# Moving the small tiles of a hybrid decoder kernel so that matmul operands and weights start at multiples of 512 bytes in SBUF

## The chip, the cores and the metric

The kernel runs on one NeuronCore of a Trainium2 chip. The metric is the device time of one execution in microseconds. The kernel before took 1934.75 us, the median of three runs (1932.48 to 1936.17).

## The reference

Two decoder layers over 256 tokens of width 2048, all in float32:

```
layer 0:  h = h + pool_mixer(rmsnorm(h))       # 4 channel groups, trailing means over 2/4/8/16 tokens, 512x512 product
          h = h + swiglu(rmsnorm(h))           # w_gate, w_up: 2048 x 5632; w_down: 5632 x 2048
layer 1:  h = h + diff_attention(rmsnorm(h))   # 8 heads, two softmaxes per head (128 wide), v 256 wide, ALiBi bias
          h = h + swiglu(rmsnorm(h))
out = rmsnorm(h)
diff_attention: a = softmax(q1 k1) - lam * softmax(q2 k2);  o = rmsnorm(a v) * subln_g * (1 - lambda_init);  o w_o
lam = exp(lq1 . lk1) - exp(lq2 . lk2) + lambda_init
```

## The kernel before

**The products.** Every large product is made of float32r matmuls of 128x128 stationary and up to 512 moving columns. An operand is held as a high and a low float32r part, and a product is three matmuls: high x high, high x low, low x high. Weights come from HBM as tiles `raw` of 128 x 4 x 512 floats, 1 MB each, by SP's queue (`load`, L102). ScalarE casts a tile to `whi`, VectorE subtracts to `wlo` (`halves`, L107). Three buffers of each of the three exist, so that loads and casts run some tiles ahead of TensorE.

**group (L130)** does a run of weight tiles into PSUM banks. A plain step multiplies the two 128-column blocks of one weight tile's four quarters with the operand tile: 24 matmuls of 512 moving columns at L164, the activation tile stationary, the weight moving. A step in `SEVEN` (three of the eight w_gu steps) uses seven products in place of eight: VectorE makes sums of the weight quarters (`tsum`, L116 to L119), ScalarE and VectorE split them to `thi` and `tlo` (L122, L123), and 21 matmuls follow, 12 of them with thi or tlo.

**The stages.** The start loads x, computes the pooling mixer and its square sums. Each FFN goes in three chunks of 4, 4 and 3 groups of 512 columns: w_gu (stationary: xq, tiles named xp in the trace), then transposes of h (L361) and the split into the tiles named h (`h0_0` to `h3_1`), then w_down with the h tiles stationary. Attention computes q and k of head after head in `product` (L418 with 512 moving columns, L420 with 256; here the weight is stationary and xp moves), scores and softmax, then w_v (xp stationary), the value products, and w_o with the tiles oT stationary.

**Where tiles lie.** A pool's tiles are laid one after the other in SBUF in the order in which they are first asked for, each place rounded up to 32 bytes; the pools `const`, `resid`, `wraw`, `whl` and `tmp` follow one another, and the pools of a stage (`start`, `ffn0`, `attn`, `ffn1`) begin where they end. So a small tile moves all that comes after it. `const` holds gain_sb (384 bytes a partition), subln_sb (8), lam_sb (16), dist_sb (1024), ident and ones (512 each). Of the tile `warm`, which ScalarE alone writes, there are two buffers in `tmp`.

**The order of the work.** The framework's scheduler orders each engine's instructions ahead of the run, from dependences and priorities in the order of the code. SP issues its loads in the order so found; a load waits until its buffer is free.

Of the kernel before, what the change touches and what calls it, by code (L numbers as in the profile page):

```python
# [9 lines left out]
F32 = mybir.dt.float32  # L10
# [6 lines left out]
P = 128  # L17
S = 256
# [26 lines left out]
def trunk_kernel(ctx, tc, x_t, x_n, gains, scale_in, final_in, subln, lam_in, band, dist,  # L45
# [10 lines left out]
    nc = tc.nc  # L56

    const = ctx.enter_context(tc.tile_pool(name="const", bufs=1))
# [3 lines left out]
    tmp = ctx.enter_context(tc.tile_pool(name="tmp", bufs=2))  # L62
# [14 lines left out]


    gain_sb = const.tile([P, 6, NK], F32, name="gain_sb")
    subln_sb = const.tile([P, 2], F32, name="subln_sb")  # L80
    lam_sb = const.tile([P, 4], F32, name="lam_sb")
    dist_sb = const.tile([P, 2 * P], F32, name="dist_sb")
    ident = const.tile([P, P], F32, name="ident")
    ones = const.tile([P, P], F32, name="ones")
# [113 lines left out]
    def rsqrt(ss, n, cols):  # L198


        v, s, t, r = (tmp.tile([P, 8], F32, name=f"rs_{x}") for x in "vstr")
        v, s, t, r = v[:, :cols], s[:, :cols], t[:, :cols], r[:, :cols]
        nc.vector.tensor_scalar(v, ss, 1.0 / n, EPS, ALU.mult, ALU.add)
        nc.scalar.activation(s, v, AF.Sqrt)
        nc.vector.reciprocal(s, s)
        nc.vector.tensor_tensor(t, s, s, ALU.mult)
        nc.vector.scalar_tensor_tensor(t, t, -0.5, v, ALU.mult, ALU.mult)
        nc.vector.scalar_tensor_tensor(r, t, 1.5, s, ALU.add, ALU.mult)
        return r

    def square_sum(ss, t, j):

        sq = tmp.tile([P, 512], F32, name="sq", bufs=1)
        nc.scalar.activation(sq, x_tok[:, t, j * 512:(j + 1) * 512], AF.Square, accum_out=ss[:, t, j:j + 1])  # L214

    def row_scale(ss):
        tot = tmp.tile([P, 2], F32, name="ss_tot")
        nc.vector.tensor_reduce(tot, ss, AX.X, ALU.add)
        r = tmp.tile([P, 2], F32, name="r_tok", bufs=3)
        nc.vector.tensor_copy(r, rsqrt(tot, D, 2))  # L220
        return r
# [35 lines left out]
    with tc.tile_pool(name="start", bufs=1, reuse_waits="tile") as st:  # L257
# [2 lines left out]
        xf = st.tile([P, NK, S], F32, name="xf")  # L260
        nc.scalar.dma_start(out=gain_sb, in_=gains)

        warm = tmp.tile([P, 8], F32, name="warm")
        nc.scalar.activation(warm[:, 0:1], ones[:, 0:1], AF.Sqrt)
        wp = aux()
        for _ in range(WARM):
# [55 lines left out]
        r = row_scale(ss_in)  # L322
        nc.sync.dma_start(out=band_sb, in_=band)
        nc.sync.dma_start(out=scale_sb, in_=scale_in)
        nc.sync.dma_start(out=subln_sb, in_=subln)
        nc.sync.dma_start(out=lam_sb, in_=lam_in)
        nc.sync.dma_start(out=dist_sb, in_=dist)
        group_product(2)
        group_mean(0)
# [5 lines left out]
    def ffn(layer, xq, ss, seven, next_op, next_gain):  # L335
# [3 lines left out]
        with tc.tile_pool(name=f"ffn{layer}", bufs=1, reuse_waits="tile") as hp:  # L339
            g0 = 0  # L340
            for c, n in enumerate(CHUNKS):
# [6 lines left out]
                for g in range(g0, g0 + n):  # L348
                    ps = group([(xq[p], p in seven, w_gu[layer][g, p]) for p in range(NP)], hp)
                    cs = combined(ps, hp)  # L350
                    h = hp.tile([P, 2, 512], F32, name="h")
# [14 lines left out]
                for o in range(2):  # L366
                    if last and o == 1:

                        pre = tmp.tile([P, 8], F32, name="warm")
                        nc.scalar.activation(pre[:, 0:1], x_tok[:, 0, 0:1], AF.Square)  # L370
                        nc.scalar.activation(pre[:, 0:1], pre[:, 0:1], AF.Sqrt)
                    ps = group([(hp_tiles[i], False, w_down[layer][o, 2 * g0 + i]) for i in range(2 * n)])
                    cs = combined(ps, hp)
                    for b in range(2):
                        j = 2 * o + b
                        for t in range(2):
                            cols = slice(j * 512, (j + 1) * 512)
                            nc.vector.tensor_tensor(x_tok[:, t, cols], cs[t][b], x_tok[:, t, cols], ALU.add)
                            if last:
                                square_sum(ss_next, t, j)  # L380
                        if last and next_op is not None:
                            transposed(next_op, j, next_gain)
                g0 += n
            if next_op is None:

                r = row_scale(ss_next)
                for j in range(4):
                    cols = slice(j * 512, (j + 1) * 512)
                    y = hp.tile([P, 2, 512], F32, name="y", tag=f"h{j // 2}_{j % 2}")
                    for t in range(2):  # L390
# [4 lines left out]
                        out=out[:, cols].rearrange("(t p) n -> p t n", p=P), in_=y)  # L395
        return ss_next

    xp = operand()
    ss = ffn(0, xq, ss, SEVEN, xp, 3)


    ss_next = tmp.tile([P, 2, 4], F32, name="ss")
    with tc.tile_pool(name="attn", bufs=1, reuse_waits="tile") as ap_, ExitStack() as heads:
        at = heads.enter_context(tc.tile_pool(name="attn_tmp", bufs=2, reuse_waits="tile"))
        v_sb = ap_.tile([P, 2, D], F32, name="v_sb")
        r_col = row_scale(ss)
        qs_col = ap_.tile([P, 2], F32, name="qs_col")
        nc.vector.tensor_scalar(qs_col, r_col, QK_SCALE, None, ALU.mult)
        r = None
        neg_lam = None  # L410
# [31 lines left out]
        probs = None  # L442
        for h in range(H):

            qk = ap_.tile([P, 4, S], F32, name=f"qk{h}", tag="qk", bufs=8)
            for i in range(4):
                ps = product(w_qk[h * 4 + i], acts)
                if i == 1 and probs is not None:
# [87 lines left out]
        for g in range(2):  # L536
            cs = combined(group([(oT[p], False, w_o[g, p]) for p in range(NP)]))
            for b in range(2):
# [5 lines left out]
                transposed(xq, j, 4, SEVEN)  # L544

    ffn(1, xq, ss_next, SEVEN, None, None)


# [89 lines left out]
```

## Time and profile before

| | |
|---|---|
| median of three runs | 1934.75 us (1932.48 to 1936.17) |
| the profiled execution | 1936.85 us, of which the span of instructions is 1935.1 |
| mean granted TensorE clock | 0.992 of full |
| TensorE matmul busy | 1892.9 us, 8508 recorded matmuls |
| VectorE busy | 1345.3 us |
| ScalarE busy | 921.5 us |
| read from HBM | 355.39 MB, 185 GB/s |

A matmul's recorded length contains its way through the array, so the lengths of matmuls that follow each other overlap. How fast the stream runs is read from the distance between starts, in the timeline or in a window's count.

### The profile page before, as it was taken

The page shows a single profiled execution, that of the slowest core. Times are in us where ns is not written, and L with a number is a line of the kernel's source. Part 1 is how long each engine was busy: PE and PEld are TensorE (multiplying, and loading weights), DVE is VectorE, ACT ScalarE, POOL GpSimd, SP SyncE. Part 2 cuts the span into 40 slices and gives each one's busy share as a digit, 9 for nine tenths or more (in the row PEclk, how much of TensorE's full clock was granted, in tenths as well). Part 3 has the DMA queues.
Part 4 walks back from the last instruction along what each step waited for, and adds up shares of the span by engine and source line. Part 5 has one row for each costly group of instructions (what it writes and reads, how often), then busy time and mean ns, then how long its engine had stood idle before and what let it go on. Part 6 is the DMA issues. An engine that isn't in the chain of part 4 may idle for free.

```text
span 1935.1 us, 20835 instructions
## 1 busy us (share of the span) xinstructions
PE 1892.9 (98%) x8508; PEld 1528.9 (79%) x8508; DVE 1345.3 (70%) x1311; ACT 921.5 (48%) x892; POOL 0.7 (0%) x6
## 2 busy tenths in 40 slices
PE   8899999999999999999999999999999999999997
PEld 5678878888888887888887777788888888888885
DVE  5889746888557974666654356888557887468854
ACT  5555534455334545544445544555334554335542
POOL 0000000000000000000000000000000000000000
PEclk9999999999999999999999999999999999999999
DMA  7455555555555454555553354555555556565552
GB/s 281 152 196 196 196 180 193 193 196 198 193 185 207 174 210 163 177 174 177 177 186 127 135 174 155 194 195 196 197 193 196 196 176 216 178 213 196 197 194 87
DMA packets 51151, 358.83 MB, mean 185 GB/s; under 512 B 6000, under 2 KB 6256, under 8 KB 8432
## 3 DMA queue, kind: packets, MB, share of 16 engines
q1 hardware_dynamic: 50080, 355.36, 52.7%
q10 hardware_dynamic: 976, 2.15, 0.3%
q8 instruction: 66, 1.08, 0.2%
q14 instruction: 29, 0.24, 0.0%
HBM read 355.39 MB, written 2.10 MB: 185 GB/s over the span
## 4 chain that ended last, share of the span: by engine, by line
PE 93%; DVE 3%; ACT 2%; DMA 1%; issue 1%; SPq 0%; DVEq 0%; ACTq 0%
PE b L164 80%; PE b L418 6%; PE b L420 3%; PE b L361 1%; DVE wlo L111 1%; DMA x_tok<-x_n 1%; ACT whi L110 1%; PE b L299 1%; PE b L485 1%; ACT sq L214 0%; PE b L531 0%; PE b L309 0%; DVE xp L226 0%; DMA raw<-w_gu 0%; DVE y L391 0%
## 5 line engine op out<-in xcount | busy, mean ns | idle before, releaser
L111 DVE TENSOR_TENSOR wlo<-raw,whi 128x2048 fp32r<-128x2048 f32 (+1 forms) x331 | 721.4, 2183 | 367.5 <-ACT whi L110 367.3
L110 ACT CAST whi<-raw 128x2048 fp32r<-128x2048 f32 (+1 forms) x331 | 603.7, 1827 | 625.0 <-PE b L164 528.2
L164 PE MATMUL b<-whi,xp 128*128 128x512 f32 x2412 | 770.4, 393 | 6.4 <-DVE xp L226 3.9
L164 PEld LDWEIGHTS b<-whi,xp 128*128 128x128 f32 x2412 | 453.1, 188 | 106.6 <-issue 4.8
L164 PE MATMUL b<-wlo,xp 128*128 128x512 f32 x1206 | 472.1, 391 | 1.7 <-DVE wlo L111 1.6
L164 PE MATMUL b<-whi,h 128*128 128x512 f32 x1408 | 446.9, 397 | 0.0
L164 PEld LDWEIGHTS b<-whi,h 128*128 128x128 f32 x1408 | 264.0, 188 | 65.1 <-DVE h L364 2.0
L164 PE MATMUL b<-wlo,h 128*128 128x512 f32 x704 | 278.5, 396 | 0.0
L164 PEld LDWEIGHTS b<-wlo,xp 128*128 128x128 f32 x1206 | 227.1, 188 | 51.5 <-DVE wlo L111 3.0
L164 PE MATMUL b<-thi,xp 128*128 128x512 f32 x528 | 186.9, 401 | 2.1 <-ACT thi L122 2.1
L123 DVE TENSOR_TENSOR tlo<-tsum,thi 128x2048 fp32r<-128x2048 f32 x66 | 151.1, 2290 | 52.4 <-ACT thi L122 51.7
L418 PE MATMUL b<-xp,whi 128*128 128x512 f32 x512 | 183.0, 401 | 0.0
L122 ACT CAST thi<-tsum 128x2048 fp32r<-128x2048 f32 x66 | 126.2, 1912 | 99.8 <-DVE tsum L119 77.0
L164 PEld LDWEIGHTS b<-wlo,h 128*128 128x128 f32 x704 | 132.3, 188 | 31.5 <-DVE wlo L111 0.4
L420 PE MATMUL b<-xp,wlo 128*128 128x256 f32 x512 | 137.9, 280 | 0.0
L164 PEld LDWEIGHTS b<-thi,xp 128*128 128x128 f32 x528 | 96.7, 188 | 29.7 <-ACT thi L122 10.4
L418 PEld LDWEIGHTS b<-xp,whi 128*128 128x128 f32 x512 | 95.0, 188 | 19.7
L164 PE MATMUL b<-tlo,xp 128*128 128x512 f32 x264 | 105.6, 400 | 0.0
L420 PEld LDWEIGHTS b<-xp,wlo 128*128 128x128 f32 x512 | 96.6, 189 | 2.6
L164 PE MATMUL b<-whi,oT 128*128 128x512 f32 x256 | 82.7, 402 | 0.4 <-DVE xp L226 0.4
L116 DVE TENSOR_TENSOR tsum<-raw 128x1024 f32<-128x1024 f32 x66 | 80.6, 1221 | 0.6
L164 PEld LDWEIGHTS b<-tlo,xp 128*128 128x128 f32 x264 | 49.5, 188 | 14.0 <-DVE tlo L123 2.6
(122 smaller groups left out, 1022.7 us busy)
## 6 DMA issues: line engine op xcount, KB each, us to landing
raw<-w_gu SPq DMA_DIRECT2D x176, 1024.0 KB, 4.9
raw<-w_down SPq DMA_DIRECT2D x88, 1024.0 KB, 4.9
raw<-w_qk SPq DMA_DIRECT2D x32, 1024.0 KB, 4.8
raw<-w_v SPq DMA_DIRECT2D x16, 1024.0 KB, 4.9
raw<-w_o SPq DMA_DIRECT2D x16, 1024.0 KB, 4.8
raw<-pool_w SPq DMA_DIRECT2D x3, 1024.0 KB, 11.1
x_tok<-x_n SPq DMA_DIRECT2D x1, 2048.0 KB, 14.8
xf<-x_t SPq DMA_DIRECT2D x3, 512.0 KB, 11.3
```

Of the source, the lines that this page charges most:

```text
L110: nc.scalar.copy(hi[:, lo_block:], raw[:, lo_block:])
L111: nc.vector.tensor_tensor(lo[:, lo_block:], raw[:, lo_block:], f32(hi[:, lo_block:]), ALU.subtract)
L116: nc.vector.tensor_tensor(t[:, T1:T3 + 1], raw[:, B11:B22 + 1], raw[:, B12:B12 + 1].broadcast_to([P, 2, 512]), ALU.add)
L122: nc.scalar.copy(hi, t)
L123: nc.vector.tensor_tensor(lo, t, f32(hi), ALU.subtract)
L164: nc.tensor.matmul(ps[b], x, y[:, block], start=first, stop=(left[b] == 0))
L299: nc.tensor.matmul(zp[g][t], u, w[:, k % 4], start=(k % 4 == 0 and i == 0), stop=(k % 4 == 3 and i == 2))
L361: nc.tensor.transpose(tp[:, k, t * P:(t + 1) * P], h[:, t, (2 * i + k) * P:(2 * i + k + 1) * P], ident)
L418: big = lambda: nc.tensor.matmul(ps.rearrange("p a s -> p (a s)"), hi[:, k], a.rearrange("p a s -> p (a s)"), start=(k == 0), stop=(k == N ...
L420: small = lambda: nc.tensor.matmul(ps[:, 0, :], lo[:, k], a[:, 0, :], start=False, stop=False)
L485: nc.tensor.matmul(sc[:, :nk], qk[:, c, qb * P:(qb + 1) * P], qk[:, 2 + c, :nk], start=True, stop=True)
```

## The change

The two small tiles subln_sb and lam_sb leave the pool `const` and are made in the pool of the attention stage, behind the first of the eight qk buffers and qs_col; their two loads are issued there in place of at the start. The first qk tile is asked for before qs_col, so that the eight qk places (used again for oT) start the part of the pool behind v_sb. The tile `warm` has one buffer.

```diff
--- before.py
+++ after.py
@@ -77,8 +77,6 @@
 
 
     gain_sb = const.tile([P, 6, NK], F32, name="gain_sb")
-    subln_sb = const.tile([P, 2], F32, name="subln_sb")
-    lam_sb = const.tile([P, 4], F32, name="lam_sb")
     dist_sb = const.tile([P, 2 * P], F32, name="dist_sb")
     ident = const.tile([P, P], F32, name="ident")
     ones = const.tile([P, P], F32, name="ones")
@@ -260,7 +258,7 @@
         xf = st.tile([P, NK, S], F32, name="xf")
         nc.scalar.dma_start(out=gain_sb, in_=gains)
 
-        warm = tmp.tile([P, 8], F32, name="warm")
+        warm = tmp.tile([P, 8], F32, name="warm", bufs=1)
         nc.scalar.activation(warm[:, 0:1], ones[:, 0:1], AF.Sqrt)
         wp = aux()
         for _ in range(WARM):
@@ -322,8 +320,6 @@
         r = row_scale(ss_in)
         nc.sync.dma_start(out=band_sb, in_=band)
         nc.sync.dma_start(out=scale_sb, in_=scale_in)
-        nc.sync.dma_start(out=subln_sb, in_=subln)
-        nc.sync.dma_start(out=lam_sb, in_=lam_in)
         nc.sync.dma_start(out=dist_sb, in_=dist)
         group_product(2)
         group_mean(0)
@@ -366,7 +362,7 @@
                 for o in range(2):
                     if last and o == 1:
 
-                        pre = tmp.tile([P, 8], F32, name="warm")
+                        pre = tmp.tile([P, 8], F32, name="warm", bufs=1)
                         nc.scalar.activation(pre[:, 0:1], x_tok[:, 0, 0:1], AF.Square)
                         nc.scalar.activation(pre[:, 0:1], pre[:, 0:1], AF.Sqrt)
                     ps = group([(hp_tiles[i], False, w_down[layer][o, 2 * g0 + i]) for i in range(2 * n)])
@@ -404,7 +400,12 @@
         at = heads.enter_context(tc.tile_pool(name="attn_tmp", bufs=2, reuse_waits="tile"))
         v_sb = ap_.tile([P, 2, D], F32, name="v_sb")
         r_col = row_scale(ss)
+        qk = ap_.tile([P, 4, S], F32, name="qk0", tag="qk", bufs=8)
         qs_col = ap_.tile([P, 2], F32, name="qs_col")
+        subln_sb = ap_.tile([P, 2], F32, name="subln_sb")
+        nc.sync.dma_start(out=subln_sb, in_=subln)
+        lam_sb = ap_.tile([P, 4], F32, name="lam_sb")
+        nc.sync.dma_start(out=lam_sb, in_=lam_in)
         nc.vector.tensor_scalar(qs_col, r_col, QK_SCALE, None, ALU.mult)
         r = None
         neg_lam = None
@@ -442,7 +443,8 @@
         probs = None
         for h in range(H):
 
-            qk = ap_.tile([P, 4, S], F32, name=f"qk{h}", tag="qk", bufs=8)
+            if h:
+                qk = ap_.tile([P, 4, S], F32, name=f"qk{h}", tag="qk", bufs=8)
             for i in range(4):
                 ps = product(w_qk[h * 4 + i], acts)
                 if i == 1 and probs is not None:
```

The first byte of the tiles in a partition, modulo 512, as the built programs have it:

| tiles | before | after |
|---|---|---|
| raw, whi, wlo; all xp and xq; x_tok; ident, ones | 64 | 0 |
| tsum, thi, tlo; h and the h tiles of w_down; band_sb, z, w0, x0; v_sb; e | 96 | 0 |
| qk and oT | 128 | 0 |
| aT | 256 | 224 |
| q_c, k_s, bias, s_sb | 256 | 224 |

Every row or block that a matmul reads lies at a multiple of 512 bytes behind the start of its tile in the products of L164 and L418, so the table holds for the operands as well.

The scheduler's order changes at two places. SP's queue at the start, before (a row is line, operation, tile written and read, shape, count):

```order
L317 DMA x_tok<-x_n 128x4096
L323 DMA band_sb<-band 128x1536
L324 DMA scale_sb<-scale_in 128x2048
L325 DMA subln_sb<-subln 128x2
L326 DMA lam_sb<-lam_in 128x4
L327 DMA dist_sb<-dist 128x256
L104 DMA raw<-pool_w 128x2048
```

SP's queue there after the change, with the line numbers of the changed kernel:

```order
L315 DMA x_tok<-x_n 128x4096
L321 DMA band_sb<-band 128x1536
L322 DMA scale_sb<-scale_in 128x2048
L323 DMA dist_sb<-dist 128x256
L102 DMA raw<-pool_w 128x2048
```

The two small loads are gone from between scale_sb and dist_sb, and the third load of pool_w is two places further up.

SP's queue around the attention stage after the change; before, the 32 loads of w_qk stand there without a break:

```order
L102 DMA raw<-w_gu 128x2048 x24
L102 DMA raw<-w_down 128x2048 x12
L102 DMA raw<-w_qk 128x2048 x5
L406 DMA subln_sb<-subln 128x2
L408 DMA lam_sb<-lam_in 128x4
L102 DMA raw<-w_qk 128x2048 x27
```

The small loads now go out behind the fifth load of w_qk.

VectorE at the end of the first FFN, before (lp and gs are what lam_sb and subln_sb are read for):

```order
L378 TENSOR_TENSOR x_tok<-b_5070,x_tok 128x512
L459 TENSOR_TENSOR lp<-lam_sb 128x2
L467 TENSOR_SCALAR gs<-subln_sb 128x2
L477 TENSOR_SCALAR bias<-dist_sb 128x256 x2
L111 TENSOR_TENSOR wlo<-raw,whi 128x2048
L226 SCALAR_TENSOR_TENSOR xp<-b_5233,gain_sb,xp 128x256
```

VectorE there after the change:

```order
L224 SCALAR_TENSOR_TENSOR xp<-b_5253,gain_sb,xp 128x256
L216 TENSOR_REDUCE ss_tot<-ss 128x2
L461 TENSOR_TENSOR lp<-lam_sb 128x2
L469 TENSOR_SCALAR gs<-subln_sb 128x2
L201 TENSOR_SCALAR rs_v<-ss_tot 128x2
```

lp and gs stand ten operations later, behind the two of bias, the wlo of a weight tile, six splits of xp and ss_tot. At the start, one split of xp (out of four) on ScalarE and VectorE stands one place earlier, ahead of a square sum and of an addition to x_tok. Elsewhere each engine's order is what it was.

## Rows read from the trace of the kernel before

**Rows 1.** The page of the profile, part 1: busy time of each engine, its share of the span, and its instructions.
```profile
PE 1892.9 (98%) x8508; PEld 1528.9 (79%) x8508; DVE 1345.3 (70%) x1311; ACT 921.5 (48%) x892; POOL 0.7 (0%) x6
```

**Rows 2.** The page, part 4: the chain of work that ended last, its shares by engine.
```profile
PE 93%; DVE 3%; ACT 2%; DMA 1%; issue 1%; SPq 0%; DVEq 0%; ACTq 0%
```

**Rows 3.** The groups of instructions of the whole span with shapes kept apart: line, engine, operation, tiles, shapes and count, then busy time in us, the mean of one in ns, and the engine's idle time before them in us. Lines of other groups stand where the dots are.
```profile
L164 PE MATMUL b<-whi,xp 128*128 128x512 f32 x2412 | 770.4, 393 | 6.4 <-DVE xp L226 3.9 <-ACT whi L110 1.7 <-ACT xp L250 0.7
L164 PE MATMUL b<-wlo,xp 128*128 128x512 f32 x1206 | 472.1, 391 | 1.7 <-DVE wlo L111 1.6
...
L164 PE MATMUL b<-whi,h 128*128 128x512 f32 x1408 | 446.9, 397 | 0.0
L164 PE MATMUL b<-wlo,h 128*128 128x512 f32 x704 | 278.5, 396 | 0.0
...
L164 PE MATMUL b<-thi,xp 128*128 128x512 f32 x528 | 186.9, 401 | 2.1 <-ACT thi L122 2.1
...
L164 PE MATMUL b<-tlo,xp 128*128 128x512 f32 x264 | 105.6, 400 | 0.0
...
L164 PE MATMUL b<-whi,oT 128*128 128x512 f32 x256 | 82.7, 402 | 0.4 <-DVE xp L226 0.4
L164 PE MATMUL b<-wlo,oT 128*128 128x512 f32 x128 | 51.1, 399 | 0.0
```

**Rows 4.** Three windows (us from the span's start), with the instructions of line L164 alone: length, busy time and count of TensorE's matmuls and of its weight loads, granted clock, DMA share, GB/s.
```profile
1000.00:1028.00 28.00, 28.00 (x125) 23.09 (x123) 1.00 0.60 221
250.00:320.00 70.00, 70.00 (x302) 56.36 (x301) 1.00 0.56 195
1112.00:1138.00 26.00, 26.00 (x113) 20.97 (x112) 1.00 0.59 201
```

**Rows 5.** A window over four whole groups of w_gu in the first FFN, all engines: length, then busy time (and count) of matmuls, weight loads, VectorE, ScalarE and POOL, granted clock, DMA share, GB/s.
```profile
328.37:499.26 170.89, 170.89 (x757) 139.04 (x756) 143.29 (x117) 88.93 (x64) 0.00 (x0) 1.00 0.56 197
```

**Rows 6.** The timeline of TensorE at transposes inside a w_gu group: start and length in us, instruction and count (equal ones that follow each other are one row).
```profile
415.98 0.82 PE L361 MATMUL b<-ident,h 128*128 128x128 f32 x6
416.55 0.48 PE L164 MATMUL b<-tlo,xp 128*128 128x512 f32 x1
416.87 0.39 PE L164 MATMUL b<-thi,xp 128*128 128x512 f32 x1
```

**Rows 7.** The timeline of TensorE in w_v, columns as in Rows 6. Between the dots the rows of one and of two take turns without a break.
```profile
1000.02 0.61 PE L164 MATMUL b<-whi,xp 128*128 128x512 f32 x2
1000.47 0.39 PE L164 MATMUL b<-wlo,xp 128*128 128x512 f32 x1
...
1003.42 0.61 PE L164 MATMUL b<-whi,xp 128*128 128x512 f32 x2
```

**Rows 8.** The same in w_o.
```profile
1120.13 0.63 PE L164 MATMUL b<-whi,oT 128*128 128x512 f32 x2
1120.60 0.40 PE L164 MATMUL b<-wlo,oT 128*128 128x512 f32 x1
...
1123.63 0.63 PE L164 MATMUL b<-whi,oT 128*128 128x512 f32 x2
```

**Rows 9.** The same in w_gu, where whi gives way to thi.
```profile
152.65 0.39 PE L164 MATMUL b<-whi,xp 128*128 128x512 f32 x1
152.87 0.40 PE L164 MATMUL b<-thi,xp 128*128 128x512 f32 x1
153.11 0.39 PE L164 MATMUL b<-tlo,xp 128*128 128x512 f32 x1
153.34 0.40 PE L164 MATMUL b<-thi,xp 128*128 128x512 f32 x1
```

**Rows 10.** The same at the pooling product of the start, in plain float32; one product is two recorded passes.
```profile
54.87 1.02 PE L309 MATMUL b<-z,band_sb 128*128 128x512 f32 x2
55.73 1.02 PE L311 MATMUL b<-z,band_sb 128*128 128x512 f32 x2
```

**Rows 11.** The same in the QK products; L418 has 512 moving columns, L420 has 256. The two lines take turns between the dots.
```profile
799.80 0.40 PE L418 MATMUL b<-xp,whi 128*128 128x512 f32 x1
800.04 0.28 PE L420 MATMUL b<-xp,wlo 128*128 128x256 f32 x1
...
801.92 0.40 PE L418 MATMUL b<-xp,whi 128*128 128x512 f32 x1
```

**Rows 12.** What TensorE waited for between 75 and 1935 us: total in us, times, longest.
```profile
PE b L164 <- ACT thi L122: 2.1, 2, 1.1
PE b L164 <- ACT whi L110: 1.7, 2, 1.1
```

**Rows 13.** The timeline of SP's queue (the DMA issues) at the start.
```profile
8.82 0.33 SPq L325 DMA_DIRECT2D subln_sb<-subln  x1
...
13.83 0.33 SPq L104 DMA_DIRECT2D raw<-pool_w  x1
```

**Rows 14.** The timeline of VectorE at the start of the attention layer.
```profile
789.63 0.15 DVE L459 TENSOR_TENSOR lp<-lam_sb 128x2 f32<-128x2 f32 x1
```

**Rows 15.** The timeline of SP's queue there: the fifth load of w_qk.
```profile
787.74 0.33 SPq L104 DMA_DIRECT2D raw<-w_qk  x1
```

**Rows 16.** The page, part 6: DMA issues of one kind, KB each, median us from issue to landing.
```profile
raw<-w_qk SPq DMA_DIRECT2D x32, 1024.0 KB, 4.8
```

## Prediction

> **What bounds the kernel now.** I read the busy times first. The reader is to see that TensorE is busy for 98% of the span while VectorE has 70% and ScalarE 48% [rows 1], and that 93% of the chain that ended last is TensorE [rows 2]. So a change pays here only if it shortens TensorE's own stream, and by as much as the stream shrinks, unless another engine then comes last. Its waits on the casts after the start come to 2.1 and 1.7 us [rows 12], so there is little waiting to win.
>
> The second view is the list of matmul groups with shapes kept apart [rows 3]. All eight groups of L164 are the same instruction (128x128 stationary, 512 columns moving), yet the mean of one is 391 to 393 ns with xp and whi/wlo, 396 and 397 with h, 399 to 402 with oT, and 400 and 401 with thi/tlo. The recorded time of one contains its latency, so the distance between starts has to be read elsewhere.
>
> The third view is the timeline in steady stretches. In w_v, with xp stationary, a triple (whi twice, wlo once) starts every 0.68 us: from 1000.02 to 1003.42 are fifteen matmuls in 3.40 us, 226.7 ns each [rows 7]. In w_o, with oT stationary and the same code, fifteen take from 1120.13 to 1123.63, 3.50 us, 233.3 ns each [rows 8]. The windows say the same over longer stretches of this line alone (a window counts every matmul that touches it, so it is its length plus one matmul of 0.39 us, over the count): 28.39 over 125 is 227 ns with xp, 70.39 over 302 is 233 ns with h, 26.39 over 113 is 233 ns with oT, all at a granted clock of 1.00, the 2.4 GHz level [rows 4]. A move from whi to thi shows it without any pause: whi to thi starts 0.22 us apart, then thi to tlo 0.24 and tlo to thi 0.23 [rows 9].
>
> Shape, type, PSUM banks, engine and clock are the same in these stretches, and DMA shares are 0.56 to 0.60. What differs is the address. By the table of addresses the pairs that run at 226.7 ns lie at the same place modulo 512 (xp at 64, whi and wlo at 64). The slow ones don't: h at 96 against 64, oT at 128 against 64, thi and tlo at 96 against xp's 64. I read this as one rule: a matmul and the weight load that runs beside it get along when their two addresses agree modulo 512, and lose 6.67 ns when they don't.
>
> **Step 1, the products that now disagree.** After the change all of them lie at 0, so they agree. The counts are in [rows 3]. With h: 1408 + 704 = 2112 matmuls x 6.67 ns = 14.1 us. With thi and tlo: 528 + 264 = 792 x 6.67 = 5.3 us. With oT: 256 + 128 = 384 x 6.67 = 2.6 us. All lie on TensorE, which is the path.
>
> The Trainium skill ("TensorE: Matmul & The Clock Gate", Step-by-step: what each phase is for) says that TensorE has two independent SBUF read ports and that loading the next weights steals no read bandwidth from the running matmul. By that rule addresses would be nothing and this step 0; the trace disagrees, since only the address separates 226.7 from 233.3 ns [rows 7, 8].
>
> **Step 2, the way back.** After a run of thi and tlo the whi/wlo matmuls don't fall to 226.7 ns at once. One stretch of four w_gu groups takes 170.89 us [rows 5]. Its 732 matmuls of L164 at 226.7 ns would be 165.9; 144 of them are with thi/tlo, 1.0 us of step 1. Its 24 transposes cost 0.11 us each (from 415.98 to 416.87 are six of them and one product of 0.23 [rows 6]), 2.6 us. 1.4 us are left for the way back and for waits. There are 22 such groups, so 0 to 7.7 us; I take half, 3.9 us, since the breaks by transposes stay.
>
> **Step 3, new breaks.** Also h and oT products will take some matmuls to settle after a pause or a transpose. Step 2 gives 0.7 us for four groups full of breaks; w_down and w_o have few, and I take back 1.0 us.
>
> **Step 4, attention's QK products.** xp is moving and whi/wlo stationary there, already at 64 and 64, so the relation does not change and I put 0. Six pairs (512 and 256 columns) take from 799.80 to 801.92, 0.353 us a pair [rows 11]. For the bounds I need a pace without any loss: the float32 products run as two passes of 512 columns at 0.43 us each [rows 10], half of which, an estimate, is 0.215 for one fp32r matmul. A pair without loss would be 0.323; with the loss of the good state (0.0117) twice 0.346, of the bad one (0.0183) twice 0.359. Over 512 pairs that is from 3.6 us gained to 3.1 lost.
>
> **Step 5, the two small loads and what they move past.** At the start subln and lam leave SP's queue between scale_sb and dist_sb, so dist_sb and the third pool_w load can be issued up to two transfers earlier (subln was issued at 8.82 and pool_w at 13.83 [rows 13]). The queue is one stream, and the two transfers are 2 and 4 values a partition, so the landing moves by tenths of a microsecond. ScalarE takes one xp activation, VectorE one xp operation, before an x_tok step. I put 0, with 1 us either way. In attention SP now issues the two behind five w_qk loads. In the old run the fifth went out at 787.74 [rows 15], and VectorE reads lam at 789.63 [rows 14]; the new order lets it read after ss_tot, some 6 us later, behind a load that takes 4.8 us [rows 16]. SP's wait for TensorE is for the last reader of h0_0, whose place the two tiles take: the first of six steps in the second half of the last w_down block, five steps of 24 matmuls (28 us) before the block's end. The next w_qk load waits for a raw buffer anyway. Cost 0. The single warm buffer is written by ScalarE alone, in order: 0.
>
> **Sum.** 14.1 + 5.3 + 2.6 + 3.9 - 1.0 = 24.9 us. The profiled execution took 1936.85 us, 2.1 over the median of the three runs, so about 1912 for its like and **1910 us** against the median of 1934.75. What is late next: in w_gu VectorE has 143.29 of 170.89 us [rows 5] and the wait for ScalarE's thi is already among the waits [rows 12]; half of thi's 5.3 us could turn into waiting there. With that, no way back, 3.1 us in QK and 1 at the start the bad end is 1920; with the whole way back, 3.6 in QK and the start the good end is 1901.
>
> **The rivals.**
> *No change (0.10).* The slow groups would be slow for another reason than the address, or the stream gets faster and TensorE waits for VectorE instead. For it: VectorE's 84% in w_gu, and that h, oT and thi are all written shortly before use. Against it: xp is as well, and in w_down VectorE and ScalarE have slack. Time: 1931 to 1938 us.
>
> *Everything disagrees (0.09, slower).* What counts may be the place itself, not the difference: 64 is an odd multiple of 64, and 96 and 128 are not. Address 0 is then like oT's 128, and all pairs run at 233.3 ns. The 2412 + 1206 matmuls with xp [rows 3] lose 6.67 ns, 24.1 us, of which about 3.9 are lost already; nothing is gained elsewhere. Time: 1955 us. It decides from the first w_v stretch: 233 instead of 227 ns. For it: no pair of the old run has both operands at 0. Against it: thi at 96 with xp at 64 is slow although xp is at the good place, which a difference explains with one rule and places need two for.
>
> *Better than the good state (0.09).* A weight row of 512 bytes at 64 runs across a multiple of 512, a row at 0 doesn't. If the 0.0117 us of step 4 that even good pairs lose come from that, all 6906 matmuls of L164 win them too, 81 us on top. Time: 1829 us. The Trainium skill (the same page, Back-to-back issue gap) puts an isolated matmul at N/2.4 + 2.5 ns, 216 for 512 columns; the trace is 11 ns above it even in its best stretch [rows 7].
>
> **The numbers.** My forecast has 0.72, with 1901 to 1920 as its own range. About 0.2%, 4 us, is what a measurement of this kernel can tell from no change. The range that holds the time 8 times in 10 is the forecast's own and the no-change case, 1901 to 1937; it leaves out the other two. Faster by over 0.2%: the forecast and the better state, 0.81. Within 0.2%: 0.10. Slower: 0.09.
>
> **What would show it.** Step 1: fifteen matmuls of a w_down and of a w_o stretch in 3.40 us, and the means of the h, oT and thi groups at about 390 ns. Step 2: the whi and wlo means with xp down by 1 to 2 ns, and four w_gu groups in about 169 us. Step 4: QK pairs still at 0.353. Step 5: no new wait for lam or subln on VectorE, and a start that is neither longer nor shorter by over 1 us. I am wrong if w_down stays at 233 ns (the address is not the cause), if w_v rises to 233 (place, not difference), or if any of them falls below 226.

## The result, and the profile after

The changed kernel takes 1915.51 us (median of five runs, 1915.21 to 1915.97) against 1933.85 (1932.47 to 1936.17) of the kernel before, run beside it: 18.3 us less, a ratio of 0.9905 with a 95% interval of 0.9891 to 0.992. The forecast was 1910, with 1901 to 1937 as its range. The two profiled executions, 1936.85 and 1915.97 us, differ by 20.9 us. In the changed kernel L164 is L162, L361 is L357, L418 and L420 are L419 and L421, and thi and tlo are made in L120 and L121.

TensorE's busy time fell by 21.2 us [rows 1], VectorE's and ScalarE's by under half a microsecond; the chain that ended last is still TensorE's [rows 2]. Part 1 of the page and the shares of part 4 after the change:

```profile
PE 1871.7 (98%) x8508; PEld 1526.5 (80%) x8508; DVE 1344.9 (70%) x1311; ACT 921.3 (48%) x892; POOL 0.7 (0%) x6
```

```profile
PE 93%; DVE 3%; ACT 2%; DMA 1%; issue 1%; SPq 0%; DVEq 0%; ACTq 0%
```

The groups of matmuls with shapes kept apart (busy us, mean ns of one, idle before them) after the change, as [rows 3]:

```profile
L162 PE MATMUL b<-whi,xp 128*128 128x512 f32 x2412 | 768.4, 392 | 6.5 <-DVE xp L224 3.9 <-ACT whi L108 1.7 <-ACT xp L248 0.7
L162 PE MATMUL b<-wlo,xp 128*128 128x512 f32 x1206 | 470.7, 390 | 1.8 <-DVE wlo L109 1.8
L162 PE MATMUL b<-whi,h 128*128 128x512 f32 x1408 | 438.3, 391 | 0.0
L162 PE MATMUL b<-wlo,h 128*128 128x512 f32 x704 | 274.2, 390 | 0.1
L162 PE MATMUL b<-thi,xp 128*128 128x512 f32 x528 | 185.1, 397 | 2.4 <-ACT thi L120 2.3
...
L162 PE MATMUL b<-tlo,xp 128*128 128x512 f32 x264 | 105.4, 399 | 0.0
...
L162 PE MATMUL b<-whi,oT 128*128 128x512 f32 x256 | 81.5, 397 | 0.5 <-DVE xp L224 0.5
L162 PE MATMUL b<-wlo,oT 128*128 128x512 f32 x128 | 50.4, 394 | 0.0
```

The products with h fell from 397 and 396 to 391 and 390, about all that was forecast. Those with thi and tlo fell only from 401 and 400 to 397 and 399: here the result is less than the forecast. The means with oT, 397 and 394, also stay above the 390 of the prediction, but these two groups contain a stretch of low clock around 1094 us; their pace, which the timeline below shows, is the one forecast. The steady stretches show the pace itself. Windows of L162 alone after the change, in w_down and w_o, columns as in [rows 4]:

```profile
250.00:320.00 70.00, 70.00 (x311) 57.95 (x310) 1.00 0.58 198
1100.00:1126.00 26.00, 26.00 (x116) 21.52 (x116) 1.00 0.58 198
```

70.39 us (the window and one matmul) over 311 are 226 ns where they were 233 over 302 [rows 4], at the same granted clock and nearly the same DMA share. The timeline of TensorE in w_o has fifteen matmuls in 3.40 us, the 226.7 ns that only w_v had before [rows 7, 8]:

```profile
1110.03 0.62 PE L162 MATMUL b<-whi,oT 128*128 128x512 f32 x2
1110.48 0.39 PE L162 MATMUL b<-wlo,oT 128*128 128x512 f32 x1
...
1113.43 0.62 PE L162 MATMUL b<-whi,oT 128*128 128x512 f32 x2
```

By stage (from first matmul to first matmul of the next, the last block to the start of its last matmul, in us, read from the traces; the columns E3 and E2 are experiments below, with the old and the new places; the 1.0 us that step 3 took back is in no row of the forecast):

| stage | forecast | before | after | gain | E3, old | E2, new | gain |
|---|---|---|---|---|---|---|---|
| start | 0 | 47.5 | 47.1 | 0.5 | 47.6 | 46.3 | 1.3 |
| w_gu, six stretches | 9.2 | 967.3 | 964.1 | 3.2 | 967.3 | 963.0 | 4.3 |
| w_down, four blocks | } | 363.1 | 353.7 | 9.4 | 363.1 | 353.7 | 9.4 |
| w_down, last | } 14.1 | 68.2 | 66.5 | 1.7 | 68.1 | 66.4 | 1.7 |
| w_down, third, and QK | } | 265.1 | 263.8 | 1.3 | 265.1 | 265.3 | -0.2 |
| w_v | 0 | 107.1 | 104.4 | 2.7 | 104.3 | 104.4 | -0.1 |
| w_o | 2.6 | 103.8 | 101.9 | 1.9 | 103.8 | 101.6 | 2.2 |

The 2.7 us of w_v are not what the new places gave. Its steady pace was 226.7 ns before; what differs is that TensorE waited and then ran two stretches at low clock in the profile before, around 1040 and 1047 us. All engines between 1046 and 1050 us, before and after, where the changed kernel is some 9 us further on in its work (length, busy time and count of matmuls, weight loads, VectorE, ScalarE, POOL, granted clock, DMA share, GB/s):

```profile
1046.00:1050.00 4.00, 3.93 (x13) 3.19 (x14) 1.62 (x4) 1.70 (x5) 0.00 (x0) 0.63 0.00 0
```

```profile
1046.00:1050.00 4.00, 4.00 (x20) 3.30 (x19) 2.29 (x1) 1.83 (x2) 0.00 (x0) 1.00 0.78 262
```

The old kernel's matmuls of 512 columns there start 0.42 to 0.43 us apart, the 1.2 GHz level. E3 has the old places and no such stretch in w_v, and its w_v takes 104.3. The profile after has one more elsewhere, in the first w_gu stretch of layer 1, behind 4.5 us in which TensorE was busy for 2.77 and waited, above all for thi. So this w_gu stretch got 0.8 us longer, while in E2 it is 0.8 us shorter than in E3:

```profile
1201.00:1205.50 4.50, 2.77 (x12) 1.67 (x10) 1.96 (x2) 4.19 (x3) 0.00 (x0) 1.00 0.68 233
1205.50:1209.50 4.00, 4.00 (x11) 3.16 (x12) 3.97 (x4) 0.00 (x0) 0.00 (x0) 0.57 0.18 31
```

So E3 against E2 is the better ruler for single stages. The start is left out: with the same old places it takes 46.7 us in one run below (E5) and 47.6 in another (E3).

### The profile page after: what moved, and what is told of

Its sections match the earlier page's. It is cut to its first block, busy times and chain, and to the rows that moved or that the text cites. A ratio compares the mean times of both kernels' runs of the same rounds, so it can differ in the third digit from the quotient of the medians.

```text
span 1914.2 us, 20836 instructions
## 1 busy us (share of the span) xinstructions
PE 1871.7 (98%) x8508; PEld 1526.5 (80%) x8508; DVE 1344.9 (70%) x1311; ACT 921.3 (48%) x892; POOL 0.7 (0%) x6
## 4 chain that ended last, share of the span: by engine, by line
PE 93%; DVE 3%; ACT 2%; DMA 1%; issue 1%; SPq 0%; DVEq 0%; ACTq 0%
PE b L162 80%; PE b L419 6%; PE b L421 3%; PE b L357 1%; DVE wlo L109 1%; ACT whi L108 1%; DMA x_tok<-x_n 1%; PE b L297 1%; PE b L487 1%; ACT sq L212 0%; PE b L533 0%; PE b L307 0%; DVE xp L224 0%; DMA raw<-w_gu 0%; ACT o_sq L525 0%
## 5 line engine op out<-in xcount | busy, mean ns | idle before, releaser
L162 PE MATMUL b<-whi,xp 128*128 128x512 f32 x2412 | 768.4, 392 | 6.5 <-DVE xp L224 3.9
L162 PEld LDWEIGHTS b<-whi,xp 128*128 128x128 f32 x2412 | 453.2, 188 | 104.4 <-issue 5.1
L162 PE MATMUL b<-wlo,xp 128*128 128x512 f32 x1206 | 470.7, 390 | 1.8 <-DVE wlo L109 1.8
L162 PE MATMUL b<-whi,h 128*128 128x512 f32 x1408 | 438.3, 391 | 0.0
L162 PEld LDWEIGHTS b<-whi,h 128*128 128x128 f32 x1408 | 263.7, 188 | 56.8 <-DVE h L360 2.1
L162 PE MATMUL b<-wlo,h 128*128 128x512 f32 x704 | 274.2, 390 | 0.1
L162 PEld LDWEIGHTS b<-wlo,xp 128*128 128x128 f32 x1206 | 226.9, 188 | 50.0 <-DVE wlo L109 3.0
L121 DVE TENSOR_TENSOR tlo<-tsum,thi 128x2048 fp32r<-128x2048 f32 x66 | 151.1, 2290 | 52.6 <-ACT thi L120 51.7
L162 PE MATMUL b<-thi,xp 128*128 128x512 f32 x528 | 185.1, 397 | 2.4 <-ACT thi L120 2.3
L419 PE MATMUL b<-xp,whi 128*128 128x512 f32 x512 | 183.1, 402 | 0.0
L120 ACT CAST thi<-tsum 128x2048 fp32r<-128x2048 f32 x66 | 126.1, 1910 | 99.5 <-DVE tsum L117 77.0
L162 PEld LDWEIGHTS b<-wlo,h 128*128 128x128 f32 x704 | 132.2, 188 | 27.3 <-DVE wlo L109 0.5
L421 PE MATMUL b<-xp,wlo 128*128 128x256 f32 x512 | 138.0, 280 | 0.0
L162 PEld LDWEIGHTS b<-thi,xp 128*128 128x128 f32 x528 | 97.2, 189 | 28.7 <-ACT thi L120 10.9
L419 PEld LDWEIGHTS b<-xp,whi 128*128 128x128 f32 x512 | 95.0, 188 | 19.8
L162 PE MATMUL b<-tlo,xp 128*128 128x512 f32 x264 | 105.4, 399 | 0.0
L421 PEld LDWEIGHTS b<-xp,wlo 128*128 128x128 f32 x512 | 96.6, 189 | 2.6
L162 PE MATMUL b<-whi,oT 128*128 128x512 f32 x256 | 81.5, 397 | 0.5 <-DVE xp L224 0.5
L162 PEld LDWEIGHTS b<-tlo,xp 128*128 128x128 f32 x264 | 50.0, 189 | 13.7 <-DVE tlo L121 3.2
```

What stands on the lines that cost most here:

```text
L120: nc.scalar.copy(hi, t)
L121: nc.vector.tensor_tensor(lo, t, f32(hi), ALU.subtract)
L162: nc.tensor.matmul(ps[b], x, y[:, block], start=first, stop=(left[b] == 0))
L419: big = lambda: nc.tensor.matmul(ps.rearrange("p a s -> p (a s)"), hi[:, k], a.rearrange("p a s -> p (a s)"), start=(k == 0), stop=(k == N ...
L421: small = lambda: nc.tensor.matmul(ps[:, 0, :], lo[:, k], a[:, 0, :], start=False, stop=False)
```

## The experiments

### E1 and E2: is it agreement, or the multiple of 512?

Both take the kernel before and add the single warm buffer and the early qk0 (the two rows under E1). E2 also pads `const`.

```diff
# E1 (and E2)
-        warm = tmp.tile([P, 8], F32, name="warm")
+        warm = tmp.tile([P, 8], F32, name="warm", bufs=1)
...
+        qk = ap_.tile([P, 4, S], F32, name="qk0", tag="qk", bufs=8)
         qs_col = ap_.tile([P, 2], F32, name="qs_col")
...
# E2 alone
+    pad = const.tile([P, 112], F32, name="pad")
```

> The kernel before with one warm buffer and the first qk tile ahead of qs_col: every operand and weight tile then lies at 64 modulo 512, none at a multiple of 512, and the two small loads stay at the start. Theory 'agreement' (a matmul and the weight load beside it only have to agree modulo 512): w_down, w_o and thi/tlo run at 226.7 ns as in the changed kernel, time 1913 to 1918 us. Theory 'place' (multiples of 512 themselves are what helps): no gain where h, oT and thi are at 64, time 1930 to 1936 us.

> The kernel before with a pad of 448 bytes in const, one warm buffer and the first qk tile ahead of qs_col: all tiles at multiples of 512 as in the changed kernel, but the two small loads stay at the start of SP's queue. If the addresses are the whole gain: 1914 to 1917 us. If moving the loads gave or cost part of it: away from 1915.5 by that part, 1 to 3 us, and the difference stands in the first 50 us.

Measured: E1 1916.82 us (ratio 0.9913, 0.9898 to 0.9928), E2 1916.22 (0.9909, 0.9894 to 0.9923). With no operand at a multiple of 512, E1 has the whole gain; its w_down blocks take 88.45 us and w_o 101.6. The places need only agree. E1's products with whi and h, and E2's window in w_down:

```profile
L164 PE MATMUL b<-whi,h 128*128 128x512 f32 x1408 | 438.4, 391 | 0.0
```

```profile
250.00:320.00 70.00, 70.00 (x311) 57.96 (x310) 1.00 0.60 202
```

One thing stays open: in both, the wide QK matmul starts its successor after 235.6 ns, against 232.9 before and after, so that their QK stage is 1.5 us longer, with the differences of whi, wlo and xp as they were.

### E3: the moved loads alone

```diff
# from the changed kernel
+    pad = const.tile([P, 16], F32, name="pad")
...
-        warm = tmp.tile([P, 8], F32, name="warm", bufs=1)
+        warm = tmp.tile([P, 8], F32, name="warm")
...
-        qk = ap_.tile([P, 4, S], F32, name="qk0", tag="qk", bufs=8)
         qs_col = ap_.tile([P, 2], F32, name="qs_col")
+        qk = ap_.tile([P, 4, S], F32, name="qk0", tag="qk", bufs=8)
```

> The changed kernel with the two loads in the attention stage, but a pad of 64 bytes in const, two warm buffers and qs_col ahead of the first qk tile, which puts all tiles back to 64, 96 and 128 modulo 512. Addresses alone matter: 1932 to 1937 us, like before. The moved loads matter: away from 1934 by 1 to 3 us.

Measured: 1934.25 us, ratio 1.0004 (0.9995 to 1.0014). The new order of the loads is worth nothing that can be told from noise. Line L163 (L164 of before) in w_down is back at 301 in 70 us:

```profile
250.00:320.00 70.00, 70.00 (x301) 56.38 (x300) 1.00 0.56 195
```

### E4: which modulus

```diff
# from the changed kernel: 128 bytes ahead of the tiles of ffn0, 256 of ffn1, 384 in attn
+            shift = hp.tile([P, 32 * (layer + 1)], F32, name="shift")
...
+        shift = ap_.tile([P, 96], F32, name="shift")
```

> The changed kernel with the tiles of the first FFN's pool (thi, tlo, h) shifted to 128, those of the second FFN's to 256 and v_sb, qk and oT to 384 modulo 512, weights and xp at 0. Read stage by stage. If agreement must be modulo 512: w_down takes about 90.8 us for 384 matmuls in both layers and w_o its 103.8, time 1930 to 1938 us. If modulo 256: the second FFN keeps 88.4 us, the first goes to 90.8, time 1923 to 1928 us. If modulo 128: all keep the gain, 1914 to 1918 us.

Measured: 1924.59 us, ratio 0.9949 (0.9932 to 0.9965). L162 in w_down of the first FFN, of the second, and in w_o:

```profile
250.00:320.00 70.00, 70.00 (x303) 56.73 (x302) 1.00 0.57 195
1372.00:1442.00 70.00, 69.37 (x305) 56.86 (x304) 1.00 0.54 187
1110.00:1136.00 26.00, 26.00 (x113) 20.90 (x113) 1.00 0.60 202
```

A shift of 128 or 384 loses the gain and one of 256 keeps it: blocks of 90.45 us in the first FFN and 88.47 in the second (the second window holds a pause of 0.63 us, hence 305). The prediction's "modulo 512" is modulo 256. And 70.39 over 303 is 232.3, not 233.1: a shift of 128 costs a little less than one of 32. The matmuls with thi and tlo, which E4 moves too, start 231.8 and 232.5 ns apart in the first FFN (shift of 128) and 228.8 and 228.9 in the second (256).

### E5: does VectorE hold the missing gain of w_gu?

```diff
# on both kernels; the low part of the weight sums is left out, thi is read in its place
-        lo = pool.tile([P, 4, 512], F32R, name="tlo")
         nc.scalar.copy(hi, t)
-        nc.vector.tensor_tensor(lo, t, f32(hi), ALU.subtract)
-        return hi, lo
+        return hi, hi
```

> The kernel before without VectorE's subtraction that makes tlo; the matmuls that read tlo read thi (their count and shapes stay, part of the low half of the seven-product steps is left out). It takes 2.29 us of VectorE from each of 66 steps, 151 us in all. It is the base of the next run. If TensorE sets the pace of w_gu alone: within 3 us of 1934. If VectorE's chain holds w_gu up here and there: 3 to 12 us below.

> The changed kernel with the same edit (tlo left out, thi read in its place). Theory 'w_gu's gain is lost to VectorE and ScalarE' : with VectorE relieved, four groups of w_gu win 1.5 to 2 us over the run before this one, where the changed kernel won 0.6 (170.89 to 170.31), and the whole gain over that run is 22 to 25 us, not 18. Theory 'the way back and thi's products were priced too high': four groups win 0.5 to 0.9 us as before, and the whole gain stays 17 to 20 us.

Measured: 1927.18 us (0.9967, 0.9957 to 0.9978) with the old places, 1908.13 (0.987, 0.9855 to 0.9884) with the new ones. The kernel with the old places is 6.3 us shorter without tlo, so VectorE's chain does hold w_gu up here and there. The gain between the two is 19.05 us, against 18.3 with tlo. Four w_gu groups fall from 170.99 to 169.95, between what the two theories had. But all six stretches of w_gu gain 5.9 us (960.5 to 954.5), where E3 against E2 gains 4.3; the whole time can hide it, since the two profiles have different stretches of low clock in w_v and w_o (w_v 108.6 and 106.1 us, w_o 102.5 and 104.5). So tlo holds some 1.6 us of w_gu's gain, read from one profile each.

### E6: the offset alone

No decoder: runs of 96 fp32r matmuls of one shape (fp32r is the table's float32r), all in one execution, the stationary block at byte s of its tile and the moving one at byte m of another, two tiles that start at the same place modulo 512.

```python
for k in range(count):
    s, m, n = steps[k % len(steps)]
    nc.tensor.matmul(ps[:, 0:n], slim[:, s // 4:s // 4 + P], wide[:, m // 4:m // 4 + n], ...)
```

> No decoder at all: 28 runs of 96 fp32r matmuls (97 in the mixed ones) each, one stationary block of 128 columns and one moving block of 512 or 256 columns, whose first bytes are chosen in two wide tiles; the output is a copy of the input. Names: agree has both at 0; sa to sn have the stationary block at 4, 8, 16, 32, 64, 96, 128, 192, 256, 320, 384, 448, 480 and 512 bytes and the moving one at 0; ma to md have the moving block at 32, 64, 128 and 256 and the stationary one at 0; ba to be have both at 4, 16, 32, 96 and 256; ha has 256 columns and both at 0, hb the stationary one at 64; pa alternates 512 and 256 columns at 0, pb the same with the stationary one at 64. Theory 'agreement': agree, ba to be and sn start every 226.7 ns, sd to sm and ma to md every 233.3. Theory 'place': sn and agree at 226.7, ba to be at 233.3. If a smaller period is enough, one of sg, si, sk is at 226.7 too. Mixed: pa at 0.353 us a pair as in the QK products, or lower if the transposes and scores around them are what holds them there.

Groups of this kernel, columns as in [rows 3]: both at 4; stationary at 32; stationary at 8; moving at 64; both at 32; moving at 256; stationary at 512; stationary at 256:

```profile
L77 PE MATMUL ba<-wide,slim 128*128 128x512 f32 x96 | 23.0, 399 | 0.0
...
L77 PE MATMUL sd<-wide,slim 128*128 128x512 f32 x96 | 22.6, 395 | 0.0
...
L77 PE MATMUL sb<-wide,slim 128*128 128x512 f32 x96 | 22.3, 393 | 0.0
L77 PE MATMUL mb<-wide,slim 128*128 128x512 f32 x96 | 22.1, 391 | 0.0
...
L77 PE MATMUL bc<-wide,slim 128*128 128x512 f32 x96 | 21.9, 389 | 0.0
L77 PE MATMUL md<-wide,slim 128*128 128x512 f32 x96 | 21.9, 389 | 0.0
L77 PE MATMUL sn<-wide,slim 128*128 128x512 f32 x96 | 21.9, 389 | 0.0
L77 PE MATMUL si<-wide,slim 128*128 128x512 f32 x96 | 21.9, 389 | 0.0
```

Start to start over the last 64 of each run, in ns, by s - m modulo 256:

| s - m | 0 | 32 | 64 | 96 | 128 | 192 | 224 |
|---|---|---|---|---|---|---|---|
| s at it, m = 0 | 226.7 | 233.3 | 233.3 | 234.3 | 232.3 | 228.9 | |
| s at it + 256, m = 0 | 226.7 | | 233.3 | | 232.4 | 228.8 | 233.3 |
| s = 0, m below it | 226.7 | | | | 232.3 | 228.9 | 233.3 |

Three ways to the same difference give the same pace. That covers all groups of the kernel before: h is at 32 against its weights, oT at 64, thi and tlo at 224 (233.3 each), and E4's 128 at 232.3. Of the offsets tried, only agreement at multiples of 32 has 226.7: both at 4 give 237.7, both at 16 give 231.1. Each run has one block of weights, so whether a matmul's own weights count or the next one's, loaded beside it, E6 doesn't tell.

### E7: do the transposes hold it?

```diff
# on both kernels; h isn't transposed
-                        tp = aux((P, 2, S))
-                        for k in range(2): ... nc.tensor.transpose(tp[...], h[...], ident)
-                        nc.scalar.copy(ht[:, :, 0], tp)
-                        nc.vector.tensor_tensor(ht[:, :, 1], tp, f32(ht[:, :, 0]), ALU.subtract)
+                        hs = h[:, :, i * S:(i + 1) * S]
+                        nc.scalar.copy(ht[:, :, 0], hs)
+                        nc.vector.tensor_tensor(ht[:, :, 1], hs, f32(ht[:, :, 0]), ALU.subtract)
```

> The kernel before without the transposes of h in w_gu: the h tiles of w_down are filled from h as it lies (so h isn't transposed, which this kernel leaves out); ScalarE's cast and VectorE's subtraction stay, with h in SBUF as their source. It is the base of a pair with the old places (64, 96, 128). Estimate from the trace: 22 groups x 8 transposes x about 0.11 us are 19 us less on TensorE, so 1910 to 1920 us, and 164 to 169 us for the four w_gu groups that take 170.9 with the transposes. Both theories expect the same of this one.

> The same edit on the changed kernel (all places at 0). In question is why w_gu gained 0.6 to 1.0 us per four groups where the prediction had 1.0 (thi, tlo) + 0.7 (way back) = 1.7. Theory A: the breaks by the transposes hold it, since after each of them some matmuls run slower whatever the addresses are. Then the pair without transposes gains 1.4 to 1.7 us per four groups, thi and tlo settle at 226.7 to 227.3 ns in place of 228.5, and the whole gain of the pair is 20 to 23 us. Theory B: part of the gain turns into waiting for the splits of VectorE and ScalarE. Then the gain per four groups stays at 0.6 to 1.0 or falls, since TensorE without transposes asks for its weights sooner, and the pair gains 16 to 19 us.

Measured: 1912.47 us (0.9892, 0.9875 to 0.9908) and 1891.91 (0.9782, 0.9767 to 0.9796), 20.6 us apart where the kernels with transposes are 18.3 apart. The stretches of four w_gu groups fall by 1.0 to 1.3 us, and all 22 groups by 6.4 in place of 4.3. thi and tlo, old places, then new:

```profile
L164 PE MATMUL b<-thi,xp 128*128 128x512 f32 x528 | 185.5, 400 | 1.1 <-ACT thi L122 1.1
...
L164 PE MATMUL b<-tlo,xp 128*128 128x512 f32 x264 | 104.2, 395 | 0.0
```

```profile
L162 PE MATMUL b<-thi,xp 128*128 128x512 f32 x528 | 182.5, 394 | 1.2 <-ACT thi L120 1.1
...
L162 PE MATMUL b<-tlo,xp 128*128 128x512 f32 x264 | 103.1, 390 | 0.0
```

The 20.6 us lie in theory A's range and thi and tlo come near its pace, 227.45 ns, but both theories miss the groups: A had 1.4 to 1.7 per four of them, B at most 1.0. The transposes hold some 2 us of the gain, not all that was missing.

### E8 and E9: can the QK pairs win too?

A QK pair took 0.353 us in the stretch of [rows 11]. E8 is E6's loop with pairs and blocks of 512 and 256 columns, again in one execution.

> A stretch of its own in place of the decoder (its output is a copy of an input): runs of 96 or 97 float32r matmuls of 512 and 256 columns, stationary at an offset against the moving operand, alone, in pairs as in the QK products, and in blocks of 2, 4 and 8 of each width. In question: why a QK pair takes 0.353 us although the widths alone sum to 226.7 + 120.0 = 346.7 ns with equal addresses, and 226.7 + 117.8 = 344.5 if the 512 wide one agrees and the 256 wide one is 64 bytes off. Theory A: the loss depends on the difference of addresses modulo 256 of a matmul and its own weights, so the mixed pair gives 344 to 347 ns and blocks of 8 the same. Theory B: it depends on the next matmul's weights, which are loaded while this one runs; in a pair the wide matmul runs beside the narrow one's weights, so a pair with the narrow one's weights off by 64 bytes loses on the wide one (351 to 355) and a pair with the wide one's weights off costs the narrow one alone. Theory C: changing the width is what costs, whatever the addresses; then all pairs stay at 353 and blocks of 8 fall to 344 to 347 per pair.

Start to start of a pair in ns. Both weights at 0: 353.3. Narrow one off by 32, 64, 96, 128, 192, 224: 346.7, 353.3, 351.7, 350.0, 346.7, 353.3. Wide one off by 64: 350.0; by 192: 340.0. Blocks of 2, 4 and 8 of each width: 347.5 to 350.8. The 256-column matmul alone takes 120.0 at 0 and 117.3 to 120.0 elsewhere. None of the three theories foresaw 340.0, so the rule for one width doesn't tell what a mixed pair does. E9 puts that pair into the kernel; E10 takes 64 instead.

```diff
# from the changed kernel; at is 48 (E9) or 16 (E10) floats for QK, 0 elsewhere
-    def halves(raw, lo_block=0):
-        hi = whl.tile([P, 4, 512], F32R, name="whi")
+    def halves(raw, lo_block=0, at=0):
+        hi = whl.tile([P, 2112], F32R, name="whi")[:, at:at + 2048].rearrange("p (b n) -> p b n", b=4)
...
-    ones = const.tile([P, P], F32, name="ones")
+    ones = const.tile([P, 8], F32, name="ones")     # read as a broadcast; makes the room
```

> The changed kernel, with every operand at 32 modulo 256 (a whi place is 256 bytes longer, the tile ones is one column and read as a broadcast), except that the QK products use whi 192 bytes into its place: the wide matmul's stationary lies 192 bytes off its moving operand modulo 256, the narrow one's 0. Theory A, the stretches of pairs carry over: such a pair took 340.0 ns in place of 353.3, so 512 pairs win 13.3 ns each, 6.8 us, less what the waits of the stage take back: 1908 to 1911 us against 1915.5, and the QK pairs in the timeline at 0.340. Rival B: the QK products read 16 different xp tiles and 16 weight blocks and stand beside casts and softmax work, and a pair stays at 0.353: 1914 to 1918 us. If multiples of 512 rather than 256 were needed, it would be above 1920.

> The same kernel with the QK products' whi 64 bytes into its place. In the stretch of pairs this took 350.0 ns in place of 353.3. Theory A: 512 x 3.3 ns = 1.7 us less than the changed kernel, 1913 to 1915 us, with pairs at 0.350. Theory B, that only being off matters and not by how much, has it as fast as the one with 192. Rival: pairs at 0.353, 1914 to 1918 us.

Measured: E9 1912.95 us (0.9888, 0.9873 to 0.9904), E10 1916.77 (0.9909, 0.9895 to 0.9923). E9's timeline of TensorE in QK, six pairs in 2.04 us where [rows 11] had 2.12:

```profile
801.23 0.39 PE L419 MATMUL b<-xp,whi 128*128 128x512 f32 x1
801.45 0.28 PE L421 MATMUL b<-xp,wlo 128*128 128x256 f32 x1
...
803.27 0.39 PE L419 MATMUL b<-xp,whi 128*128 128x512 f32 x1
```

0.340 us, as E8 had it. E10's undisturbed pairs (starts under 260 ns apart) take 350.0 on the mean, but the changed kernel's take 350.2 and not E8's 353.3, so E10 shows no gain. The third w_down block and QK take 260.8 us in E9, 263.6 in E10 and 263.8 in the changed kernel. E9's time lies between the ranges of its two theories. The estimate of 6.8 us came out at 3.0: E9's undisturbed pairs run at 343.7 on the mean, since each product's first pairs and those beside transposes are slower, and those of the changed kernel, at 350.2, had less to lose than E8's. E9 is the fastest version here. Its interval overlaps that of the changed kernel, so in the whole time 2.6 us between them is not settled; the stage's 3.0 us are read from one profile each.

## Why the prediction was right, and where it was not

**What bounds the kernel** held. TensorE's stream sets the time, and 18.3 us came from its pace. The cause named, two addresses that agree or don't, was right: the same instruction with nothing but an offset changed runs at 226.7 or 233.3 ns in E6. That the loss arises between a matmul and the weight load that runs beside it is still argued: no run has matmuls without weight loads. The Trainium skill ("TensorE: Matmul & The Clock Gate", Step-by-step: what each phase is for) says the weight load takes no read bandwidth from a running matmul; if nothing else tied the two, the place of the weights would not count, and E6 has 6.7 ns in 226.7 by it.

**Step 1** was right for h and oT. h: 14.1 forecast, 12.4 from the w_down blocks of E3 and E2 (1.4 of it in the third). Start to start the mean of the undisturbed matmuls fell from 233.32 to 226.95 ns. oT: 2.6 forecast, 1.9 (2.2 in E2). The rule's modulus was wrong, 256 and not 512; here that changes no number, since 32 and 64 differ from 0 by either. That one loss of 6.67 ns served for all three was luck of the old places: E6 has 233.3 ns at 32, 64 and 224, but 232.3 at 128 and 228.9 at 192.

**The term that was mis-sized is w_gu**: thi and tlo of step 1 (5.3) and the way back of step 2 (3.9), 9.2 us together, came to 3.2 in the profiles and 4.3 in E3 against E2. The missing 6.0 us of the profiles have three parts, which add up within rounding.
- By pace the trace shows 6.9: over the starts in w_gu that are under 260 ns apart, xp with whi and wlo went from 227.92 to 226.92 (3029 of them, 3.0 us: the way back is nearly gone), thi and tlo from 233.31 to 228.53 (3.0 us, if it is counted for all 630), and the changes between the two kinds give 0.9. So the pace itself fell 2.3 us short, at thi and tlo, whose runs the transposes of h and waits break up. After the change, with starts and lengths in us:

```profile
151.74 0.39 PE L162 MATMUL b<-whi,xp 128*128 128x512 f32 x1
151.97 0.39 PE L162 MATMUL b<-thi,xp 128*128 128x512 f32 x1
152.19 0.39 PE L162 MATMUL b<-tlo,xp 128*128 128x512 f32 x1
...
153.10 0.38 PE L357 MATMUL b<-ident,h 128*128 128x128 f32 x2
153.24 0.71 PE L162 MATMUL b<-thi,xp 128*128 128x512 f32 x2
153.79 0.40 PE L162 MATMUL b<-tlo,xp 128*128 128x512 f32 x1
```

  whi to thi to tlo now goes on at 0.22 to 0.23 [rows 9]; after the transposes two thi take 0.55. Such a break cost the same before: where at least five thi and tlo follow one (eight times), the five distances behind the first add up to 1.246 us before and 1.245 after, so these gain nothing from agreement. Without transposes (E7) thi and tlo settle at 227.45 and w_gu gains 6.4.
- 2.4 us became waiting, by which three waits of the weight loads grew, before and after (us in total, times, longest):

```profile
PEld b L164 <- ACT thi L122: 10.4, 24, 1.5
...
PEld b L361 <- DVE h L355: 5.0, 20, 0.4
...
PEld b L164 <- DVE tlo L123: 2.6, 10, 0.4
```

```profile
PEld b L162 <- ACT thi L120: 10.9, 24, 1.5
...
PEld b L357 <- DVE h L351: 6.3, 20, 0.4
...
PEld b L162 <- DVE tlo L121: 3.2, 12, 0.4
```

  Most of it is for h and tlo, not for thi as the prediction had it. A stream that gets ahead of its producers waits for them: E5, without tlo, gains 1.6 us more in w_gu.
- 1.4 us is the stretch of low clock in layer 1 (180.2 us, 178.7 in E2). E2 has the same places without it, so the places alone don't bring it; why this profile has it stays open.

The stated bad end (half of thi's 5.3 us turned into waiting, no way back) has 2.7 us for w_gu, nearer to the 3.2 and 4.3 measured than the 9.2 taken, but for another reason: the way back came, and the gain of thi and tlo did not. The prediction had put the breaks in w_down and w_o at 1.0 us (**step 3**), without saying that they also cut the gain of thi and tlo. How much of E7's 2.1 and E5's 1.6 us is the same time no run shows, and together they fall short of the 4.9 us that E3 against E2 leaves missing.

**Step 4** was right at 0: the narrow and wide starts are 117.25 and 232.90 ns, 117.16 and 232.91 before. That E9 finds 3.0 us there, near the bound of 3.6, is luck: it comes by a difference of 192, and the bound was worked out for the relation that the change leaves as it is. **Step 5** was right (E3).

**The rivals.** *No change* is out by the interval. *Everything disagrees* is out: the pace in w_v is as before, and E1 shows that the place is not what counts. *Better than the good state* is out for 512 columns: no offset in E6 went below 226.7.

## What to carry to other kernels

When the same matmul runs at two paces in one kernel, read start-to-start distances by operand and set the SBUF addresses beside them, before looking for waits. Put stationary and moving operands of fp32r products of 512 columns at the same place modulo 256, at multiples of 32; a pad in an early pool moves everything behind it, for the better or the worse. Price the gain of a faster stream by what its producers allow, and measure pace and stage apart, since a stretch of low clock is as large as such a term.

## What the runs showed of the hardware

- The pace of a stream of fp32r matmuls of 512 columns depends on s - m (stationary less moving address) modulo 256 and is not symmetric: 64 ahead costs 6.7 ns, 64 behind (192) costs 2.2 (E6).
- With 256 columns agreement is among the slow cases: 120.0 ns at 0, 128 and 160, against 117.3 at 96 and 118.3 at 32 (E8).
- A pair of 512 and 256 columns takes 340.0 to 353.3 ns by the offset of its weights, and the fastest has its wide matmul in disagreement (E8, E9).
- Agreement at 4 bytes (237.7) is slower than every disagreement tried, at most 234.3 (E6).
- Behind transposes the first five distances of thi and tlo take as long with agreement as without it, 1.245 and 1.246 us (after, before).

Why any of these numbers is what it is no run shows.
